# Work between two experts cut into single-engine steps, and the output accumulator begun by ScalarE and VectorE instead of GpSimd

## The chip, the core and the metric

The kernel runs on one core of a Trainium2 chip. Its engines work side by side, each through its own queue in order: TensorE (PE, matrix products; its weight loads are shown as PEld), VectorE (DVE), ScalarE (ACT), GpSimd (POOL) and SyncE (SP, which issues the transfers from HBM). PE writes its products to PSUM, from where ACT and DVE read them; everything else lies in SBUF. The metric is the device time of one execution in microseconds (us), taken as the median of several runs.

## What is computed

A two-layer block over 256 tokens of width 1024. Each layer is a convolution-and-retention mixer, a layer norm, a feed-forward part and a layer norm. The feed-forward part is dense in layer 0 and a mixture of 8 experts in layer 1, where each token goes to its best two experts. The change lies in the mixture alone:

```python
ALPHA = (2.0 * DEPTH) ** 0.25
D_MODEL, D_FF, N_EXPERTS, TOP_K = 1024, 3584, 8, 2

def moe_swiglu(h, router, w1, w3, w2):          # h: 256 x 1024
    logits = jnp.einsum('nd,de->ne', h, router)
    top_logit, top_e = lax.top_k(logits, TOP_K)
    gate = jax.nn.softmax(top_logit, axis=-1)
    ...                                         # tokens of each expert gathered into xe
    a = xe @ w1[e]
    c = xe @ w3[e]
    y = (jax.nn.silu(a) * c) @ w2[e]
    ...                                         # y times its gate, summed back to its token

x = layer_norm(ALPHA * x + moe_swiglu(x, ...), ln2_g, ln2_b)
```

## The kernel before

Everything is fp32. A product is made accurate by splitting each operand into a high part (an fp32r copy, `...h`) and a low part (the rest, `...l`) and adding three matmuls (`mm3`, L154 to L156: high by high, high by low, low by high). The function `parts` does the split: ACT copies the high part (L109), then DVE, or for a few weights POOL, subtracts it from the source (L110).

The mixture takes the time from about 477 us to 1471 us of the profiled execution. It has 8 experts of 7 blocks each; (e, b) is block b of expert e. A block handles 512 of the 3584 hidden columns and reads six weight tiles of 128x2048 from HBM (`raw`), each used as two splits (`wh`, `wl`, 128x1024): splits 0 to 3 are w1, 4 to 7 are w3, 8 to 11 are w2. A split feeds six matmuls of 512 columns. The third split of a block (split 2) has its low part made by POOL, all others by DVE. In program order a block is

- `a`: four calls of `up` over splits 0 to 3, among which the block before is finished: the activation `hh` after split 0 (`act`: silu on ACT, product on DVE), its transposes `ph` on PE after split 2 (`turn`), and its parts `hth`, `htl` after split 3 (`split_h`);
- `cc`: four calls of `up` over splits 4 to 7;
- `down_prev`: four calls of `down` over splits 8 to 11, for the block before, into the two PSUM tiles `y` of the expert (pool `py`, two buffers, so the next expert's `y` needs both to be read).

`W.take()` hands out a split and, with `LOOK = 2`, first writes the `parts` of the split two further on. So ACT and DVE are some splits ahead of PE in the program, and there are four buffers of splits (`SPL`): a split's high part can be written when PE is through with the split four before it.

No scheduler reorders anything (`manual_schedule`): each engine's queue is in the order in which the Python code emits its instructions. Work that belongs to no block is held in the list `side` as Python generators. `step()` runs the first of them up to its next `yield`. Before the change a block calls `step()` three times: after `a`, after the second split of `cc`, and after `cc`. The generators are

- `combine`, appended when an expert's last `down` is emitted, which is in block (e+1, 0): for each half h of `y` it takes the parts of `y` (`ysNh`, `ysNl`), multiplies with the selection matrix `PTx` on PE for both halves of the tokens (`put`, product `pc`, 2 matmuls each), and adds the gated product into `acc` on DVE (`add`, L772). It runs in blocks 1 and 2 of the next expert.
- `tokens_of(e+1)`, appended at block 2 of the odd experts 1, 3 and 5, for the next two experts: DVE builds the selection matrix `P` (4 instructions, L742), then four times PE gathers the tokens (`pg`, 8 matmuls of 256 columns, L751) and `parts` splits the product for the two experts (`gah`/`gal`, and `gbh`/`gbl` or `gch`/`gcl`), then PE transposes `P` (L760) and ACT copies it to `PTx`.

`pc`, `pg`, `pt` and `ph` share one PSUM pool of two buffers (`ptp`). At block (1, 0) the accumulator `acc` is begun: POOL adds the two parts of x (L873, two instructions of 128x1024) and ACT multiplies by ALPHA (L874).

## Time and profile before

| | |
|---|---|
| median of 3 runs | 1488.01 us (1486.11 to 1498.08) |
| the profiled execution | 1490.48 us |
| its span, first to last instruction | 1488.7 us |
| PE busy | 1438.5 us (97%) |
| PE weight loads busy | 1208.2 us (81%) |
| DVE busy | 1234.3 us (83%) |
| ACT busy | 973.8 us (65%) |
| POOL busy | 276.1 us (19%) |
| HBM read | 433.69 MB |

Times in the rows below are microseconds from the span's start. A matmul's duration overlaps the next one's, so PE's pace is read from one start to the next. "Idle before" is the time in which the engine had nothing to do ahead of an instruction, and the arrow names what ended it.

### The profile page before, as it was taken

To read this page: it belongs to the slowest core of one execution; us is meant where nothing else is said; L and a number is where in the kernel's file an instruction comes from. 1 tells how busy PE (TensorE), PEld (TensorE's weight loads), DVE (VectorE), ACT (ScalarE), POOL (GpSimd) and SP (SyncE) were. 2 spreads that over 40 slices of the span, in tenths; PEclk is the share of its full clock that TensorE was granted. 3 is DMA by queue.
4 is the path that set the end of the run, shared out by engine and by line. 5 is a ranking of instruction groups with operands and counts; after the bars stand their busy time and mean duration, and the time that the engine had idled before them with its cause. 6 is when DMAs were issued, how large, how long until landed. Compare 5 with 4: busy or idle time off the path is not lost. (4 is left out here: it accounts for less than half of the span.)

```text
span 1488.7 us, 19729 instructions
## 1 busy us (share of the span) xinstructions
PE 1438.5 (97%) x7385; PEld 1208.2 (81%) x7385; DVE 1234.3 (83%) x1401; ACT 973.8 (65%) x1153; POOL 276.1 (19%) x138
## 2 busy tenths in 40 slices
PE   9989999999987999999999999999999999999995
PEld 8859999998856887778878877888887888888884
DVE  7976455547987899889899998999899899999896
ACT  6334344434443877768877767777877777787773
POOL 5630000002844113111111111111111111111111
PEclk9999999999997999999999999999999999999998
DMA  9535544545547888979999997999998899999951
GB/s 368 208 113 227 194 175 183 211 161 182 183 164 310 311 312 336 343 300 356 382 342 378 367 356 302 368 371 352 378 376 304 342 376 354 363 373 370 353 216 59
DMA packets 62311, 436.10 MB, mean 293 GB/s; under 512 B 7040, under 2 KB 7424, under 8 KB 9856
## 3 DMA queue, kind: packets, MB, share of 16 engines
q1 hardware_dynamic: 61920, 434.24, 77.4%
q8 instruction: 60, 0.98, 0.3%
q10 hardware_dynamic: 288, 0.52, 0.1%
q14 instruction: 43, 0.35, 0.1%
HBM read 433.69 MB, written 1.05 MB: 292 GB/s over the span
## 5 line engine op out<-in xcount | busy, mean ns | idle before, releaser
L110 DVE TENSOR_TENSOR wl<-raw,wh 128x1024 fp32r<-128x1024 f32 (+1 forms) x704 | 880.5, 1289 | 61.2 <-ACT wh L109 35.8
L109 ACT CAST wh<-raw 128x1024 fp32r<-128x1024 f32 (+1 forms) x802 | 820.8, 1045 | 160.2 <-PE ac L156 94.7
L110 POOL TENSOR_TENSOR wl<-raw,wh 128x1024 fp32r<-128x1024 f32 x98 | 241.9, 2484 | 1107.3 <-ACT wh L109 1062.5
L155 PE MATMUL ac<-wl,gah 128*128 128x512 f32 x448 | 175.2, 391 | 2.8 <-DVE wl L110 2.3
L154 PE MATMUL ac<-wh,gah 128*128 128x512 f32 x448 | 177.4, 396 | 0.0
L154 PE MATMUL y<-wh,hth 128*128 128x512 f32 x440 | 172.8, 393 | 3.6 <-DVE ys1l L110 3.6
L155 PE MATMUL y<-wl,hth 128*128 128x512 f32 x440 | 172.0, 391 | 3.8 <-DVE wl L110 3.8
L156 PE MATMUL ac<-wh,gal 128*128 128x512 f32 x448 | 175.1, 391 | 0.0
L156 PE MATMUL y<-wh,htl 128*128 128x512 f32 x448 | 174.5, 390 | 0.0
L154 PE MATMUL wk<-xh,wh 128*128 128x256 f32 x512 | 145.4, 284 | 1.8 <-ACT wh L109 1.8
L156 PE MATMUL wk<-xh,wl 128*128 128x256 f32 x512 | 145.0, 283 | 0.2 <-DVE wl L110 0.2
L155 PE MATMUL wk<-xl,wh 128*128 128x256 f32 x512 | 144.7, 283 | 0.0
L391 DVE SCALAR_TENSOR_TENSOR wk<-u,colt,wk 128x256 f32<-128x256 f32 x209 | 99.8, 489 | 5.7
L154 PEld LDWEIGHTS y<-wh,hth 128*128 128x128 f32 x440 | 82.6, 188 | 24.3 <-DVE ys1l L110 6.6
L155 PEld LDWEIGHTS ac<-wl,gah 128*128 128x128 f32 x448 | 84.4, 188 | 21.4 <-DVE wl L110 3.6
L155 PEld LDWEIGHTS y<-wl,hth 128*128 128x128 f32 x440 | 82.6, 188 | 22.4 <-DVE wl L110 5.6
L154 PEld LDWEIGHTS wk<-xh,wh 128*128 128x128 f32 x512 | 97.4, 190 | 3.4 <-ACT wh L109 2.2
L156 PEld LDWEIGHTS wk<-xh,wl 128*128 128x128 f32 x512 | 99.1, 194 | 0.7 <-DVE wl L110 0.7
L156 PEld LDWEIGHTS ac<-wh,gal 128*128 128x128 f32 x448 | 84.3, 188 | 17.8
L156 PEld LDWEIGHTS y<-wh,htl 128*128 128x128 f32 x448 | 84.1, 188 | 17.4
L155 PEld LDWEIGHTS wk<-xl,wh 128*128 128x128 f32 x512 | 97.5, 190 | 0.9
L154 PEld LDWEIGHTS ac<-wh,gah 128*128 128x128 f32 x448 | 84.4, 188 | 16.6
(202 smaller groups left out, 2055.1 us busy)
## 6 DMA issues: line engine op xcount, KB each, us to landing
raw<-in_wm_dram SPq DMA_DIRECT2D x336, 1024.0 KB, 7.0
raw<-in_ws_dram SPq DMA_DIRECT2D x68, 1024.0 KB, 5.0
raw<-in_lnp_dram SPq DMA_DIRECT2D x4, 1024.0 KB, 5.0
raw<-in_ws_dram SPq DMA_DIRECT2D x8, 256.0 KB, 5.5
xf<-in_xT_dram SPq DMA_DIRECT2D x4, 256.0 KB, 4.7
x<-in_x_dram SPq DMA_DIRECT2D x1, 1024.0 KB, 7.5
mask<-in_mask_dram SPq DMA_DIRECT2D x1, 768.0 KB, 12.7
gn<-in_gnp_dram SPq DMA_DIRECT2D x2, 256.0 KB, 8.3
```

Source lines behind the costliest of these rows:

```text
L109: sc.copy(hi, src)
L110: (eng or v).tensor_tensor(lo, src, f32(hi), op=ALU.subtract)
L154: pe.matmul(o, a[0], b[0], start=first, stop=False, skip_group_check=True)
L155: pe.matmul(o, a[0], b[1], start=False, stop=False, skip_group_check=True)
L156: pe.matmul(o, a[1], b[0], start=False, stop=last, skip_group_check=True)
L391: v.scalar_tensor_tensor(d, u[:, cc, k:k + S], w[:, k:k + 1], o, op0=ALU.mult, op1=ALU.add)
```

## The change

The generators are cut at more places, so that a step emits work for PE alone, or for ACT and DVE alone. A block calls `step()` at six places: after `a`, after each of the first three splits of `cc`, after `cc`, and after the first split of `down_prev`. `combine` takes both halves of `y` apart in its first two steps and then alternates one `put` and one `add`. A gather step is cut between its matmuls and its `parts`. The accumulator is begun by a generator of its own, in four steps of 128x512 on ACT and DVE. `later_tokens` builds `P` in its first step and leaves the next one empty.

```diff
@@ gather
                                   skip_group_check=True)
+            yield
             for i in range(n):
                 parts(gs[i][0][:, k:k + 2, :], gs[i][1][:, k:k + 2, :], p[:, :, i, :])
             yield
...
                 pe.transpose(p[:, i, tok(t)], f32(P[:, t, 128 * i:128 * i + 128]), ident)
+        yield
         sc.copy(PT, p)
@@ combine
     def combine(y, PT, gate_of):
+
+        ys = []
         for h in range(2):
-            ys = split([128, 512], y[h], late[0], f"ys{h}")
+            ys.append(split([128, 512], y[h], late[0], f"ys{h}"))
             yield
-            ps = [put(ys, PT, t) for t in range(NT)]
+        for h in range(2):
             for t in range(NT):
-                add(ps[t], t, h, gate_of(t))
-            yield
+                p = put(ys[h], PT, t)
+                yield
+                add(p, t, h, gate_of(t))
+                yield
+
+    def start_acc():
+
+        for t in range(NT):
+            for h in range(2):
+                o = acc[:, t, half(h)]
+                sc.mul(o, f32(xn[0][:, t, half(h)]), ALPHA)
+                v.scalar_tensor_tensor(o, f32(xn[1][:, t, half(h)]), ALPHA, o, op0=ALU.mult, op1=ALU.add)
+                yield
...
+    def later_tokens(e0):
+        g = tokens_of(e0)
+        yield
+        yield
+        yield from g
@@ first gather, ahead of block (0, 0)
-    for _ in range(2):
+    for _ in range(4):
         next(g0)
@@ down_prev
             down(hp, q, W.take(), y, pb == 0, pb == NB - 1)
+            if q == 0:
+                step()
@@ block (1, 0)
-            for t in range(NT):
-                gp.tensor_tensor(acc[:, t, :], f32(xn[0][:, t, :]), f32(xn[1][:, t, :]), op=ALU.add)
-                sc.mul(acc[:, t, :], acc[:, t, :], ALPHA)
+            side.append(start_acc())
@@ blocks
-            side.append(tokens_of(e + 1))
+            side.append(later_tokens(e + 1))
...
             if not prev:
-                next(g0, 0)
+                next(g0, 0), next(g0, 0)
...
             up(cc, q, W.take(), got[e][0])
-            if q == 1:
+            if q < 3:
                 step()
         step()
```

What this does to the queues is shown at three places. The first is DVE in block (1, 1), from the parts `htl` of the block before to the activation `hh` of the next: `ys0l` and `ys1l` are the low parts of expert 0's result, `acc<-pc` the additions. Before:

```order
L110 TENSOR_TENSOR htl<-ph,hth 128x512
L110 TENSOR_TENSOR ys0l<-y,ys0h 128x512
L110 TENSOR_TENSOR wl<-raw,wh 128x1024 x2
L772 SCALAR_TENSOR_TENSOR acc<-pc,gate,acc 128x512 x2
L110 TENSOR_TENSOR wl<-raw,wh 128x1024 x2
L110 TENSOR_TENSOR ys1l<-y,ys1h 128x512
L110 TENSOR_TENSOR wl<-raw,wh 128x1024 x4
```

The same place of DVE after the change:

```order
L110 TENSOR_TENSOR htl<-ph,hth 128x512
L110 TENSOR_TENSOR ys0l<-y,ys0h 128x512
L110 TENSOR_TENSOR wl<-raw,wh 128x1024
L110 TENSOR_TENSOR ys1l<-y,ys1h 128x512
L110 TENSOR_TENSOR wl<-raw,wh 128x1024 x2
L774 SCALAR_TENSOR_TENSOR acc<-pc,gate,acc 128x512
L110 TENSOR_TENSOR wl<-raw,wh 128x1024 x2
L774 SCALAR_TENSOR_TENSOR acc<-pc,gate,acc 128x512
L110 TENSOR_TENSOR wl<-raw,wh 128x1024 x3
```

The low part `ys1l`, which frees the second `y` tile, moved up by three splits, and the two additions no longer stand together.

The second place is ACT in the gather of expert 1, blocks (1, 2) and (1, 3), from one `hth` on; `gah` and `gch` are the high parts of the gathered tokens. Before:

```order
L109 CAST hth<-ph 128x512
L109 CAST wh<-raw 128x1024 x2
L109 CAST gah<-pg 128x256
L109 CAST gch<-pg 128x256
L109 CAST wh<-raw 128x1024 x2
L109 CAST gah<-pg 128x256
L109 CAST gch<-pg 128x256
L109 CAST wh<-raw 128x1024 x5
L794 ACTIVATE hh<-ac 128x512
```

After the change, from the `hth` in block (1, 3):

```order
L109 CAST hth<-ph 128x512
L109 CAST wh<-raw 128x1024
L109 CAST gah<-pg 128x256
L109 CAST gch<-pg 128x256
L109 CAST wh<-raw 128x1024 x2
L109 CAST gah<-pg 128x256
L109 CAST gch<-pg 128x256
L109 CAST wh<-raw 128x1024 x2
L109 CAST gah<-pg 128x256
L109 CAST gch<-pg 128x256
L109 CAST wh<-raw 128x1024 x4
L809 ACTIVATE hh<-ac 128x512
```

The copies out of `pg` moved from blocks (1, 2) and (1, 3), two pairs each, to blocks (1, 3) and (1, 4), three pairs and one; on PE the eight matmuls of each pair now stand one turn (one split's six matmuls) ahead of where its copies are emitted.

The third place is the start of `acc`. On ACT before, around the boundary of blocks (0, 6) and (1, 0):

```order
L109 CAST wh<-raw 128x1024 x8
L874 ACTIVATE acc<-acc 128x1024 x2
L109 CAST wh<-raw 128x1024
L794 ACTIVATE hh<-ac 128x512
```

On DVE after the change, inside block (1, 0); ACT has a multiplication of 128x512 ahead of each, and POOL's two additions are gone from its queue:

```order
L110 TENSOR_TENSOR htl<-ph,hth 128x512
L795 SCALAR_TENSOR_TENSOR acc<-xl,acc 128x512
L110 TENSOR_TENSOR wl<-raw,wh 128x1024
L795 SCALAR_TENSOR_TENSOR acc<-xl,acc 128x512
L110 TENSOR_TENSOR wl<-raw,wh 128x1024
L795 SCALAR_TENSOR_TENSOR acc<-xl,acc 128x512
L110 TENSOR_TENSOR wl<-raw,wh 128x1024
L795 SCALAR_TENSOR_TENSOR acc<-xl,acc 128x512
L110 TENSOR_TENSOR wl<-raw,wh 128x1024 x5
```

The start moved from the block boundary, where POOL did it in two pieces, to four places between the splits 5 to 9 of block (1, 0), where DVE does it.

## Rows read from the trace of the kernel before

**Rows 1.** Windows of one block each: stretch, its us, busy PE, PEld, DVE, ACT, POOL; clock, DMA

```profile
1060.65:1077.47 16.82, 16.82 (x78) 13.91 (x77) 15.26 (x13) 13.43 (x15) 2.42 (x1) 1.00 0.94 375
575.91:595.99 20.08, 17.74 (x77) 13.67 (x76) 19.20 (x13) 13.69 (x15) 9.08 (x3) 1.00 0.83 311
595.99:613.91 17.92, 17.08 (x77) 13.83 (x76) 15.15 (x13) 14.67 (x17) 2.39 (x1) 1.00 0.95 356
1111.07:1129.59 18.52, 18.00 (x81) 14.58 (x80) 17.70 (x19) 14.24 (x17) 2.41 (x1) 1.00 0.93 343
1129.59:1151.69 22.10, 20.49 (x98) 16.39 (x97) 18.90 (x22) 14.20 (x19) 2.43 (x1) 1.00 0.78 288
1151.69:1171.97 20.28, 19.79 (x97) 16.11 (x96) 17.53 (x18) 14.74 (x20) 2.98 (x1) 1.00 0.81 312
1257.70:1275.61 17.91, 17.91 (x82) 14.58 (x81) 16.48 (x15) 13.40 (x15) 2.41 (x1) 1.00 0.92 334
```

**Rows 2.** Timeline of PE: start, us, line, operation; a gather's first matmul, the matmul behind it

```profile
643.19 0.28 PE L751 MATMUL pg<-P,xh 128*128 128x256 f32 x1
...
644.13 0.40 PE L154 MATMUL ac<-wh,gbh 128*128 128x512 f32 x1
```

**Rows 3.** Waits in the mixture: us in total, times, longest

```profile
PE y L155 <- DVE wl L110: 3.8, 6, 0.8
PE y L154 <- DVE ys1l L110: 3.6, 7, 0.5
```

**Rows 4.** Timeline of an undisturbed block: a low part on DVE, and PE's matmuls

```profile
1057.86 1.23 DVE L110 TENSOR_TENSOR wl<-raw,wh 128x1024 fp32r<-128x1024 f32 x1
1059.29 0.39 PE L154 MATMUL y<-wh,hth 128*128 128x512 f32 x1
1060.65 0.39 PE L154 MATMUL ac<-wh,gah 128*128 128x512 f32 x1
1060.88 0.39 PE L155 MATMUL ac<-wl,gah 128*128 128x512 f32 x1
1069.53 0.39 PE L155 MATMUL ac<-wl,gah 128*128 128x512 f32 x1
```

**Rows 5.** Timeline of DVE in that block

```profile
1062.01 4.43 DVE L110 TENSOR_TENSOR wl<-raw,wh 128x1024 fp32r<-128x1024 f32 x3 [0.26 <-ACT wh L109]
1066.37 0.68 DVE L110 TENSOR_TENSOR htl<-ph,hth 128x512 fp32r<-128x512 f32 x1
1066.97 3.49 DVE L110 TENSOR_TENSOR wl<-raw,wh 128x1024 fp32r<-128x1024 f32 x3
```

**Rows 6.** Timeline of ACT and DVE around a gather step in block (1, 2)

```profile
644.33 0.37 ACT L109 CAST gah<-pg 128x256 fp32r<-128x256 f32 x1 [4.65 <-PE pg L751]
644.74 0.42 DVE L110 TENSOR_TENSOR gal<-pg,gah 128x256 fp32r<-128x256 f32 x1 [1.09 <-ACT gah L109]
646.55 2.36 DVE L110 TENSOR_TENSOR wl<-raw,wh 128x1024 fp32r<-128x1024 f32 x2 [0.52 <-ACT wh L109]
```

**Rows 7.** Timeline of POOL, DVE and ACT around the start of `acc`

```profile
578.30 6.71 POOL L873 TENSOR_TENSOR acc<-xh,xl 128x1024 f32<-128x1024 f32 x2
577.27 8.82 DVE L110 TENSOR_TENSOR wl<-raw,wh 128x1024 fp32r<-128x1024 f32 x3 [0.25 <-ACT wh L109]
594.43 2.00 ACT L874 ACTIVATE acc<-acc 128x1024 f32<-128x1024 f32 x2
```

**Rows 8.** Timeline of DVE: an addition pair, two-input work in SBUF, a selection matrix

```profile
623.22 1.41 DVE L772 SCALAR_TENSOR_TENSOR acc<-pc,gate,acc 128x512 f32<-128x512 f32 x2
1483.27 2.06 DVE L1005 SCALAR_TENSOR_TENSOR acc<-acc,rsl,raw 128x512 f32<-128x512 f32 x3
472.99 0.88 DVE L742 TENSOR_SCALAR P<-iota,rk 128x128 fp32r<-128x128 f32 x4
```

**Rows 9.** Timeline of POOL: a split in an undisturbed block and in block (1, 3)

```profile
1060.68 2.42 POOL L110 TENSOR_TENSOR wl<-raw,wh 128x1024 fp32r<-128x1024 f32 x1 [14.09 <-ACT wh L109]
654.56 2.97 POOL L110 TENSOR_TENSOR wl<-raw,wh 128x1024 fp32r<-128x1024 f32 x1 [19.63 <-ACT wh L109]
```

## The prediction

> **What bounds the kernel now.** I read the windows of single blocks first [rows 1]. The undisturbed block, the first row, takes 16.82 us, all of it with PE at work and at clock 1.00, while DVE works 15.26 and ACT 13.43. So PE sets the pace, and a block that takes longer is longer by what PE was given to do in addition and by what it waited. The change adds and removes no matmul, so only waits can be won. I take the additional work out of the disturbed blocks at measured prices. A split is six matmuls and takes 1.36 (1059.29 to 1060.65) [rows 4], so one is 0.227; the four products `pc` of a block cost 0.91. A gather's eight matmuls cost 0.94 (643.19 to 644.13) [rows 2]. Four transposes cost 0.46, what 16.82 has left over 72 matmuls of 0.227. Then, by [rows 1]:
>
> - (5, 1): 18.52 - 16.82 - 0.91 = 0.79 waited
> - (5, 2), products and two gathers: 22.10 - 16.82 - 0.91 - 1.88 = 2.49
> - (5, 3), two gathers and `pt`: 20.28 - 16.82 - 1.88 - 0.46 = 1.12
> - (6, 2), products: 17.91 - 16.82 - 0.91 = 0.18; (6, 1) is like (5, 1), 0.79
> - (0, 6) 20.08 - 16.82 = 3.26 and (1, 0) 17.92 - 16.82 = 1.10, around the start of `acc`
>
> An odd and an even expert together wait 5.37. There are three such pairs (1 and 2, 3 and 4, 5 and 6), expert 7 has 0.97 without a gather, and `acc` has 4.36: 16.1 + 0.97 + 4.36 = 21.4 us in all. That is the most that the change can give, 1.4% of the time. The waits name the culprits: PE's `y` products wait for `ys1l`, once per expert, and for low parts `wl` [rows 3].
>
> **Why PE waits.** A low part is ready ahead of PE by a margin. In the undisturbed block DVE ends a `wl` at 1057.86 + 1.23 = 1059.09 and PE needs it at 1060.88: 1.79 [rows 4]. DVE makes one every 1.14 ((3.49 - 1.21) / 2) [rows 5] against PE's 1.36, so the margin regains 0.22 per split, up to 1.8. Each other DVE instruction takes its length off; each piece of extra PE work adds its own. After `htl` it is lowest: 1066.97 + 1.21 to 1069.53, 1.35 [rows 4, 5]. So a lump above 1.3 us on DVE stalls PE, and so does an engine that waits at its queue's head. The latter is the gather of before: ACT stood 4.65 before `gah`, since PE was some splits behind in the same program, and DVE 1.09 after it [rows 6].
>
> **The change, part by part.**
>
> *Combine.* The parts `ys0l` and `ys1l` now come in two turns before `down`, so the wait for `ys1l` goes. What they cost the margin: 1.35 after `htl`, less 0.60 for `ys0l` (the 0.60 that `htl` takes to the next start [rows 5]), plus 0.45 for the first product that PE does meanwhile, 1.20 for split 6; plus 0.22, less 0.60 for `ys1l`, 0.82 for split 7. An addition takes 0.66 (two end 1.41 after the first begins, the second running 0.75) [rows 8], and between two of them lie two splits (0.44) and a product (0.45), so the margin doesn't fall further. `P` takes 0.88 [rows 8] after split 9 of block 2, where it is back at 1.6. No wait is left: 0.
>
> Does an addition wait at the head of DVE's queue for its product? The product stands before split 6 on PE, the addition behind `wl` of split 8. DVE is there at the earliest 1.8 before PE needs split 8, 2.72 + 0.23 - 1.8 = 1.15 after PE is through with the product. No.
>
> *Gather.* With its matmuls a turn ahead, ACT still arrives first, but waits about 1 instead of 4.65. From PE's start on split 4, `gah` starts 0.20 later (644.13 to 644.33), `gal` 0.41 after that, the next `wl` 1.81 after that [rows 2, 6], and ends 1.21 on: 3.63. PE needs it (split 7) after three splits, one gather of 0.94 and 0.23, at 5.25: margin 1.62. Each further step stretches one interval of DVE from 1.14 to 1.14 + 1.81 = 2.95, against 1.36, and gains 0.94 on PE. Block 3 has three steps now: 1.62, 2.78 for split 8, 1.19 for split 9, 1.41, and 1.41 + 1.36 - 2.95 = -0.18 for split 11. A wait of 0.2, and I add 0.1 for the restart. What is late next is POOL's split of the next block. It has a margin of 0.5 (1060.68 + 2.42 to 1063.60, two splits behind 1060.88) [rows 4, 9], but with DVE's margin at about 0.6 there, DVE's `wl` runs 1.0 into its start, and POOL ends with it: in block (1, 3) POOL took 2.97 instead of 2.42 in that way [rows 9]. That makes 0.35 and 0.1 of restart. Together 0.8 per odd expert, 2.3 in all. Bounds: 0, if the steps overlap better than I chain them, and 13.7, if all twelve steps wait as the longest did before, 0.8 idle [rows 3] and 0.34 of restart and lost overlap. I take 2.3, nearest to rows 6, which have the same chain.
>
> *Accumulator.* POOL's two additions take 6.71, and the three `wl` of DVE beside them 8.82, 2.94 each instead of 1.14 [rows 7]; ACT's two multiplications, 2.00, hold up the cast for POOL's next split. Both go, 4.36 with them. New are four DVE instructions of two SBUF operands, 0.66 each by ((2.06 - 0.74) / 2) [rows 8], and up to 2.9 for one that meets a POOL instruction, as the `wl` in [rows 7]; POOL has one split per block, early, so they lie clear. Four turns in a row cost 0.66 - 0.22 = 0.44 of margin each: 1.35 - 0.66 = 0.69 for split 6, then 0.25, -0.19, and again below zero: two waits of 0.2 to 0.3 and two restarts of 0.1, 0.8 in all. ACT's four multiplications, half as long as those of [rows 7], 0.5 each, fit its idle time.
>
> Here the Trainium skill speaks against the change. "Perfetto Trace Analysis", section Optimizing Scalar/DVE Operations, says that where DVE is saturated, work should move off it, to Scalar or even GPSIMD; this moves the other way. The trace bears it out in part: DVE's idle time in a block is 16.82 - 15.26 = 1.56 [rows 1], less than the 2.64 that it is given. What that would make of the time is the third rival.
>
> *The rest.* The first gather's order on each engine is unchanged; the fallback for crowded experts has no row in the trace. The weights' transfers keep their order; they are hidden, no wait of PE names one.
>
> *Sum.* 21.4 - 2.3 - 0.8 = 18.3 off. The profiled execution, 1490.5 with a span of 1488.7, becomes 1472.2; the median stands 2.5 below it, 1488.0 - 18.3 = 1469.7.
>
> **The rivals.**
>
> *The gather still stalls.* For it: rows 6 show how one step blocks three queues in turn, and three steps now fall in one block instead of two. Against: the longest part of that wait, 4.65, was the distance in the program. If the twelve steps cost between what they cost now (about 2.7 per odd expert, 8.1) and 13.7 instead of 2.3, the time is 1475.5 to 1481; I set 1477.
>
> *No new waits at all.* If steps overlap, all 21.4 are won: 1466.6. Against: the chain of [rows 6] is three engines long.
>
> *The accumulator overloads DVE.* If POOL's additions were not what held DVE's `wl`, the 4.36 would stay and DVE's 2.64 come on top: 1488.0 - (21.4 - 4.36) + 2.3 + 2.6 = 1475.9. Against: the three `wl` are slow exactly while POOL adds [rows 7].
>
> *The pace of the transfers takes over.* Undisturbed blocks already move 375 GB/s at a share of 0.94 [rows 1]. If 375 were the ceiling over the whole mixture, gains would be lost in the stretches that need more; but a pair with its combines and gathers now needs 14 blocks' weights in 14 x 16.82 + 7.9, 3% below 375. A quarter of the gain lost would give 1474.
>
> *DVE waits for PE (the slower side).* Place: the 28 additions and 12 gather steps, each now behind PE work that is emitted one turn ahead. If the products come later than DVE, each wait is up to one turn, 1.36, 54 in all, of which DVE's idle time (1.56 a block [rows 1], some 20 blocks) hides 31: 1470 + 23 = 1493. It decides from 0.46 uncovered per step on (18.3 / 40). Against: 1.15 us of lead worked out above.
>
> That the change does not do what it says is excluded by the queues' order.
>
> **How the numbers follow.** Forecast (1467.5 to 1473): 0.58. Gather still stalls (up to 1481): 0.19. No new waits: 0.10. Accumulator: 0.04. Transfers: 0.04. Slower side: 0.05. A measurement tells about 1% (14.9 us, 1473.1) from no change. Forecast and no new waits lie beyond that but for a small tail: faster 0.66. Within 1%: the gather's case, accumulator, transfers, part of the last and the tail, 0.30. Slower by over 1% needs 33 us over the forecast, 0.8 per step uncovered: 0.04. The range reaches from 1466, all waits gone, to 1479, most of the gather's case; about 0.15 lies outside.
>
> **What would show it.** Right: PE's wait for `ys1l` is gone; blocks 1 and 2 of an expert take 17.7 (16.82 + 0.91), block 3 of an odd one 19.7 to 20.0 (three gathers, one wait), (0, 6) 16.8; ACT's idle time ahead of `gah` is near 1; a wait of 0.2 to 0.5 is left in blocks 3 and 4 of the odd experts and in (1, 0). Wrong: waits of about 1 in (5, 3), or DVE waiting for `pc`. The prediction falls if blocks without side work are no longer 16.8.

## The result, and the profile after

The changed kernel takes 1471.11 us in the median of 4 runs (1469.57 to 1474.45), the kernel before 1487.53 in runs beside it. The ratio is 0.9884 with a 95% interval of 0.9858 to 0.9909: 1.2% faster, as forecast (1469.7, range 1466 to 1479).

The profiled execution took 1474.45 us, its span is 1472.6, 16.1 shorter than before's. Not all of the difference between two spans belongs to the change, so I compare one stretch in both: from PE's start on block (0, 1) to its start on block (7, 6), which holds all that the change touches but the steps of the first gather. Windows of this stretch, with the columns of [rows 1], before:

```profile
491.07:1446.56 955.49, 941.87 (x4270) 772.03 (x4268) 868.89 (x788) 740.15 (x803) 139.53 (x56) 1.00 0.92 349
```

and after:

```profile
493.64:1430.52 936.88, 935.82 (x4269) 773.16 (x4268) 860.89 (x792) 740.01 (x805) 133.23 (x54) 1.00 0.93 356
```

The stretch is 18.61 us shorter, with TensorE's granted clock at 1.00 in both. The sum of the prediction was 18.3. PE's busy time is now within 1.1 us of the stretch, and DVE has less busy time than before although it was given the accumulator: its low parts no longer stand beside POOL's additions, and the three later matrices `P` take 0.86 us each, where they took 3.03 beside POOL's split. The same views of single blocks as in [rows 1], after: the undisturbed (5, 5), then (0, 6), (1, 0), (5, 1) to (5, 4), (6, 2):

```profile
1174.84:1191.65 16.81, 16.81 (x77) 13.90 (x76) 15.27 (x13) 13.39 (x15) 2.42 (x1) 1.00 0.99 381
578.46:595.25 16.79, 16.79 (x77) 13.91 (x76) 15.25 (x13) 13.40 (x15) 2.42 (x1) 1.00 0.95 353
595.25:612.63 17.38, 17.32 (x77) 13.75 (x76) 16.71 (x17) 15.05 (x19) 2.41 (x1) 1.00 0.96 362
1100.71:1118.43 17.72, 17.72 (x81) 14.66 (x80) 17.05 (x17) 14.15 (x17) 2.41 (x1) 1.00 0.92 331
1118.43:1136.13 17.70, 17.70 (x81) 14.66 (x80) 17.28 (x20) 13.42 (x15) 2.51 (x1) 1.00 0.97 364
1136.13:1156.12 19.99, 19.99 (x102) 16.67 (x101) 16.44 (x19) 14.52 (x20) 2.42 (x1) 1.00 0.89 320
1156.12:1174.84 18.72, 18.56 (x90) 15.17 (x88) 17.19 (x16) 14.58 (x19) 2.82 (x1) 1.00 0.89 351
1242.96:1260.68 17.72, 17.72 (x82) 14.65 (x80) 16.79 (x16) 13.40 (x15) 2.53 (x1) 1.00 0.95 352
```

The reader takes out the extra PE work as the prediction did. Blocks 1 and 2 of an expert are 16.81 + 0.91: no wait. (5, 3) has three gathers, 16.81 + 2.82 = 19.63, so 0.36 was waited; (5, 4) has one and the transposes, 16.81 + 0.94 + 0.46 = 18.21, so 0.51. (1, 0) waits 0.57. Two of the waits of the mixture (us in total, times, longest) that are left:

```profile
PEld y L155 <- DVE wl L110: 2.2, 6, 0.5
...
PE ac L155 <- POOL wl L110: 1.0, 4, 0.5
```

The wait for `ys1l` [rows 3] is gone. Where the 0.36 and the 0.51 lie is seen in the timeline of block (5, 3) and its end. ACT's casts of the three gather steps (in brackets the idle time before them):

```profile
1143.19 0.37 ACT L109 CAST gah<-pg 128x256 fp32r<-128x256 f32 x1 [0.81 <-PE pg L751]
1144.06 0.37 ACT L109 CAST gch<-pg 128x256 fp32r<-128x256 f32 x1 [0.49 <-DVE gal L110]
...
1146.89 0.37 ACT L109 CAST gah<-pg 128x256 fp32r<-128x256 f32 x1 [0.56 <-PE pg L751]
1148.13 0.37 ACT L109 CAST gch<-pg 128x256 fp32r<-128x256 f32 x1 [0.88 <-DVE gal L110]
...
1150.59 0.38 ACT L109 CAST gah<-pg 128x256 fp32r<-128x256 f32 x1 [0.18 <-PE pg L751]
1152.22 0.37 ACT L109 CAST gch<-pg 128x256 fp32r<-128x256 f32 x1 [1.26 <-DVE gal L110]
```

ACT waits 0.8 and less for PE, where [rows 6] had 4.65. Its second cast, `gch`, waits for DVE's `gal`, and longer from step to step, so that a step costs ACT 1.30, 1.44 and 1.44 of idle time in all. DVE's low parts behind the last of them, POOL's split, and PE's matmuls on these parts:

```profile
1153.57 3.50 DVE L110 TENSOR_TENSOR wl<-raw,wh 128x1024 fp32r<-128x1024 f32 x3 [0.52 <-ACT wh L109]
...
1156.52 2.82 POOL L110 TENSOR_TENSOR wl<-raw,wh 128x1024 fp32r<-128x1024 f32 x1 [17.95 <-ACT wh L109]
...
1154.51 0.39 PE L154 MATMUL y<-wh,hth 128*128 128x512 f32 x1
1154.85 0.50 PE L155 MATMUL y<-wl,hth 128*128 128x512 f32 x1
...
1158.85 0.39 PE L154 MATMUL ac<-wh,gbh 128*128 128x512 f32 x1
1159.39 0.50 PE L155 MATMUL ac<-wl,gbh 128*128 128x512 f32 x1 [0.16 <-POOL wl L110]
```

From L154 to L155 PE takes 0.23 when it does not wait; here it takes 0.34 at split 11 and 0.54 at POOL's split. POOL runs from 1156.52 to 1159.34, 2.82 instead of 2.42, since DVE's third `wl` lies beside its start. The matmul behind each of the two waits also starts 0.1 late (1155.19 and 1159.72, 0.34 and 0.33 behind the one that waited, instead of 0.23).

### The profile page after: what moved, and what is told of

The parts are those of the page before. It is cut to its first block, busy times and chain, and to the rows that moved or that the text cites. A ratio compares the mean times of both kernels' runs of the same rounds, so it can differ in the third digit from the quotient of the medians.

```text
span 1472.6 us, 19730 instructions
## 1 busy us (share of the span) xinstructions
PE 1436.3 (98%) x7385; PEld 1211.4 (82%) x7385; DVE 1226.3 (83%) x1405; ACT 973.6 (66%) x1155; POOL 269.6 (18%) x136
## 3 DMA queue, kind: packets, MB, share of 16 engines
HBM read 433.69 MB, written 1.05 MB: 295 GB/s over the span
## 5 line engine op out<-in xcount | busy, mean ns | idle before, releaser
L154 PE MATMUL ac<-wh,gah 128*128 128x512 f32 x448 | 177.4, 396 | 0.0
L155 PE MATMUL ac<-wl,gah 128*128 128x512 f32 x448 | 174.9, 390 | 0.5 <-POOL wl L110 0.5
L155 PE MATMUL y<-wl,hth 128*128 128x512 f32 x440 | 171.7, 390 | 0.1
L154 PE MATMUL y<-wh,hth 128*128 128x512 f32 x440 | 171.4, 389 | 0.0
L154 PE MATMUL wk<-xh,wh 128*128 128x256 f32 x512 | 145.6, 284 | 0.7 <-ACT wh L109 0.7
L155 PE MATMUL wk<-xl,wh 128*128 128x256 f32 x512 | 144.9, 283 | 0.0
L154 PEld LDWEIGHTS wk<-xh,wh 128*128 128x128 f32 x512 | 97.5, 190 | 2.4 <-ACT wh L109 1.3
L155 PEld LDWEIGHTS ac<-wl,gah 128*128 128x128 f32 x448 | 84.4, 188 | 17.7 <-POOL wl L110 0.9
L156 PEld LDWEIGHTS ac<-wh,gal 128*128 128x128 f32 x448 | 84.2, 188 | 17.9
L155 PEld LDWEIGHTS wk<-xl,wh 128*128 128x128 f32 x512 | 97.6, 191 | 0.9
L156 PEld LDWEIGHTS y<-wh,htl 128*128 128x128 f32 x448 | 84.1, 188 | 17.4
L154 PEld LDWEIGHTS ac<-wh,gah 128*128 128x128 f32 x448 | 84.5, 189 | 16.6
L155 PEld LDWEIGHTS y<-wl,hth 128*128 128x128 f32 x440 | 82.6, 188 | 18.8 <-DVE wl L110 1.9
L154 PEld LDWEIGHTS y<-wh,hth 128*128 128x128 f32 x440 | 82.6, 188 | 17.1
```

The lines of the kernel that those rows point to most:

```text
L154: pe.matmul(o, a[0], b[0], start=first, stop=False, skip_group_check=True)
L155: pe.matmul(o, a[0], b[1], start=False, stop=False, skip_group_check=True)
L156: pe.matmul(o, a[1], b[0], start=False, stop=last, skip_group_check=True)
```

## The experiments

A table first. "Stretch" is PE's time from block (0, 1) to (7, 6) as above; it leaves out what varies ahead of the mixture, so it tells apart what the medians can't.

| kernel | stretch | against the changed kernel | median, us | ratio to before |
|---|---|---|---|---|
| before | 955.49 | +18.61 | 1487.5 to 1488.6 | 1 |
| changed | 936.88 | 0 | 1471.11 | 0.9884 (0.9858 to 0.9909) |
| changed, again | 936.84 | 0.0 | 1468.44 | 0.9867 (0.9845 to 0.9890) |
| accumulator as before | 940.56 | +3.7 | 1473.74 | 0.9889 (0.9853 to 0.9926) |
| gather joined | 941.34 | +4.5 | 1474.09 | 0.9899 (0.9860 to 0.9938) |
| combine as before | 944.27 | +7.4 | 1477.40 | 0.9913 (0.9883 to 0.9943) |
| spread, one place late | 935.84 | -1.0 | 1468.34 | 0.9852 (0.9824 to 0.9880) |
| lumps added | 940.55 | +3.7 | 1471.56, one run | |
| combine joined | 937.41 | +0.5 | 1473.13, one run | |
| accumulator on POOL, cut | 938.66 | +1.8 | 1470.35, one run | |
| gather spread | 934.74 | -2.1 | 1467.07 | 0.9855 (0.9832 to 0.9877) |
| POOL forms added | 937.91 | +1.0 | 1471.67, one run | |
| places alone | 949.29 | +12.4 | 1481.80, one run | |

**The accumulator as before.** This takes back one part:

```diff
-            side.append(start_acc())
+            for t in range(NT):
+                gp.tensor_tensor(acc[:, t, :], f32(xn[0][:, t, :]), f32(xn[1][:, t, :]), op=ALU.add)
+                sc.mul(acc[:, t, :], acc[:, t, :], ALPHA)
```

> The changed kernel, but the accumulator is begun as before: two GpSimd additions and two ScalarE multiplications in one piece ahead of block (1, 0). Theory (GpSimd's additions hold up VectorE's low parts while they run, and ScalarE's multiplications hold up a cast): block (0, 6) goes back from 16.79 to 20.1 us and (1, 0) from 17.38 to 17.9, all others stay; the three low parts beside the additions take 2.9 each again; the time is 1471.1 + 3.8 = 1474.9. Rival (the accumulator's work on VectorE is what costs in the changed kernel, since VectorE is nearly full): (1, 0) falls to 16.8, (0, 6) rises by less than 0.6, the time is 1471 or less.

Windows of (0, 6) and (1, 0):

```profile
574.28:594.31 20.03, 17.68 (x77) 13.68 (x76) 19.20 (x13) 13.67 (x15) 9.08 (x3) 1.00 0.78 297
594.31:612.25 17.94, 17.09 (x77) 13.83 (x76) 15.15 (x13) 14.68 (x17) 2.39 (x1) 1.00 0.93 355
```

The timeline of DVE, its low parts beside POOL's additions:

```profile
575.64 8.83 DVE L110 TENSOR_TENSOR wl<-raw,wh 128x1024 fp32r<-128x1024 f32 x3 [0.25 <-ACT wh L109]
```

Both blocks are as in [rows 1], the three low parts take 8.83 as in [rows 7], and all else stays but (1, 2), which takes 17.70 instead of 17.83: this part of the change is worth 3.24 + 0.56 = 3.8 by the two blocks, 3.7 by the stretch, of 4.36 that the prediction gave to it before its own 0.8. The rival is out: DVE, with a busy time of 16.71 in (1, 0) of the changed kernel, carries the work at 0.57 of waiting.

**The gather joined.** The casts and subtractions go back to the step of their matmuls; an empty step keeps the matmuls where they were:

```diff
                                   skip_group_check=True)
-            yield
             for i in range(n):
                 parts(gs[i][0][:, k:k + 2, :], gs[i][1][:, k:k + 2, :], p[:, :, i, :])
             yield
+            yield
@@
-        yield
         sc.copy(PT, p)
+        yield
```

> The changed kernel, but the gather's casts and subtractions are issued in the same step as their matmuls; the matmuls stay at the same places of the block, and the copy of PT comes with its transposes. It isolates 'one engine's turn at a time' from 'more places, further apart'. Theory (ScalarE and VectorE wait at the head of their queues for the matmuls, since they are ahead of TensorE): ScalarE's idle time before a gah grows from about 1 to over 2 us, the low part behind a step comes one split earlier in need, its margin falls from 1.6 to about 0.3 at the first step and below zero at the following ones; blocks 3 and 4 of an odd expert, 38.7 together, become 40 to 42.5, and the time 1475 to 1482. Rival (only the spacing over six places matters): blocks 3 and 4 stay within 0.3 of 19.98 and 18.70, and the time within 1470 to 1472.

Windows of (5, 3) and (5, 4):

```profile
1133.94:1155.28 21.34, 20.55 (x102) 16.65 (x100) 16.71 (x19) 14.91 (x21) 2.41 (x1) 1.00 0.86 303
1155.28:1174.14 18.86, 18.76 (x90) 15.17 (x88) 16.96 (x16) 14.31 (x18) 2.98 (x1) 1.00 0.85 338
```

The timeline of ACT, the casts in (5, 3):

```profile
1141.00 0.37 ACT L109 CAST gah<-pg 128x256 fp32r<-128x256 f32 x1 [1.75 <-PE pg L751]
...
1144.70 0.37 ACT L109 CAST gah<-pg 128x256 fp32r<-128x256 f32 x1 [0.57 <-PE pg L751]
...
1148.40 0.37 ACT L109 CAST gah<-pg 128x256 fp32r<-128x256 f32 x1 [0.18 <-PE pg L751]
```

The two blocks take 40.2, the low end of the theory's 40 to 42.5 (the median of 1474.09 is just under its 1475); the rival's 38.7 is out. The theory was right on the first step (ACT idles 1.75 instead of 0.81) and wrong on the next ones, where ACT waits 0.57 and 0.18 ahead of `gah`, and 0.88 and 1.26 ahead of `gch`, as in the changed kernel. So the turn between matmuls and parts is worth 1.5 per odd expert, lost at the first step of a block, and not a wait more per step.

**The combine as before.** The order within `combine` and its places are those of before, the rest as changed:

```diff
-        ys = []
         for h in range(2):
-            ys.append(split([128, 512], y[h], late[0], f"ys{h}"))
+            ys = split([128, 512], y[h], late[0], f"ys{h}")
             yield
-        for h in range(2):
-            for t in range(NT):
-                p = put(ys[h], PT, t)
-                yield
-                add(p, t, h, gate_of(t))
-                yield
+            yield
+            ps = [put(ys, PT, t) for t in range(NT)]
+            for t in range(NT):
+                add(ps[t], t, h, gate_of(t))
+            yield
+            yield
+        yield
+        yield
```

> The changed kernel, but the combine runs as before at the places of before: ys0, then its two products with their additions two places on, ys1 two places on, its two products with their additions in the next block; the gather's steps and the accumulator stay as changed. Theory (TensorE waits for ys1l because that part is made only right before the down products need its buffer): the wait for ys1l is back, 0.8 per expert; block 1 of each expert is 18.5 instead of 17.7, block 2 within 0.2 of 17.7; seven experts give +5.5 to +7, the time is 1477 to 1478. Rival (the four additions lump by lump on VectorE were the cost, whatever the place of ys1): block 2 is longer by as much as block 1, 0.4 to 0.8 each.

Windows of (5, 1) and (5, 2):

```profile
1113.31:1131.86 18.55, 18.03 (x81) 14.58 (x80) 17.50 (x17) 14.24 (x17) 2.42 (x1) 1.00 0.96 349
1131.86:1149.78 17.92, 17.92 (x82) 14.58 (x80) 17.00 (x19) 13.44 (x15) 2.41 (x1) 1.00 0.97 358
```

PE's wait in the whole mixture (us in total, times, longest):

```profile
PE y L154 <- DVE ys1l L110: 3.8, 7, 0.7
```

The wait for `ys1l` is back in all seven experts. Block 1 is longer by 0.83, block 2 by 0.22, together 1.05 and 7.4 in all: the late `ys1l` makes four fifths of it. Most of the rest is in block 2, at the second of two products in a row, whose weight load waits 0.3 for `htl`: as the code has it, that part has to be made before the PSUM buffer of `ph` is free for the product. So the combine is 7.4 of the 18.6; the accumulator is 3.7, and the 7.5 that are left are the gather's and, as is shown further down, those of the place where `P` is built.

**The combine joined.** Only the turn between a product and its addition is taken away:

```diff
                 p = put(ys[h], PT, t)
-                yield
                 add(p, t, h, gate_of(t))
                 yield
+                yield
```

> The changed kernel, but each addition of the combine is issued in the same step as its product, with an empty step behind; the products, the splits, the gather and the accumulator stay at their places. Theory (VectorE is 1.1 us behind a product with the turn between, which is about the 1.14 us of the low part that no longer lies between): VectorE reaches the addition just as the product ends, it waits 0 to 0.3, and blocks 1 and 2 of an expert stay within 0.3 of 17.7; the time is 1471 to 1473. Rival (the turn is what the combine gains by): VectorE waits 0.5 to 1 per addition, blocks 1 and 2 become 18.2 or more, seven experts give +7, 1478.

Blocks 1 and 2 stay at 17.7 in all seven experts, and DVE waits for a product 1.0 us in 6 waits, 0.2 at the longest. Only block 3 of an odd expert is longer, 20.17 instead of 19.98, 0.5 in all. So in the combine it is the place of `ys1` that counts, not the turn between product and addition, and the slower rival (DVE at the head of its queue, waiting for PE) does not bite even without that turn.

**The places alone.** The kernel before, with the three more places for a step and nothing else:

```diff
         for q in range(4):
             down(hp, q, W.take(), y, pb == 0, pb == NB - 1)
+            if q == 0:
+                step()
@@
-            if q == 1:
+            if q < 3:
                 step()
```

> The kernel before with one part of the change alone: side work gets a turn at six places of a block instead of three; the pieces themselves are not cut, and the accumulator is as before. Theory (the places bring ys1l earlier, but put uncut pieces closer together): the wait for ys1l is gone; block 1 of an expert holds the whole combine, 16.82 + 1.81 + 0.3 to 0.6 = 19.1, block 2 of an even one is 16.8, together 35.9 against 36.5; in block 2 of an odd one all four gathers lie a split apart, 16.82 + 3.76 + 0.46 + 2 to 4 us of waits = 23 to 25, block 3 is 16.8, so an odd expert's three blocks take 59 to 61 against 60.9; in all 3 to 6 us below the kernel before, 1482 to 1485. Rival (the places are what the change gains by, the cutting is not needed): the three blocks of an odd expert take 57 or less, and the time is 1476 or less.

Windows of (5, 1) to (5, 3) and (6, 2):

```profile
1104.98:1123.83 18.85, 18.85 (x85) 15.34 (x84) 18.18 (x19) 14.26 (x17) 2.42 (x1) 1.00 0.90 339
1123.83:1147.84 24.01, 22.43 (x113) 17.86 (x112) 19.95 (x26) 15.97 (x24) 2.70 (x1) 1.00 0.69 261
1147.84:1164.84 17.00, 17.00 (x77) 13.84 (x76) 16.35 (x14) 13.35 (x15) 2.97 (x1) 1.00 0.97 386
...
1250.93:1267.76 16.83, 16.83 (x78) 13.91 (x76) 15.86 (x14) 13.41 (x15) 2.69 (x1) 1.00 0.98 383
```

The odd expert's three blocks take 59.86, the even one's two 18.85 + 16.83 = 35.7, at the short end of the theory's range; the stretch is 6.2 shorter than before's, a third of the gain. Block 1 holds the whole combine and waits 0.2 (18.85 - 16.81 - 1.82), so the `ys1l` wait is cured by the place alone. Block (5, 2) holds all four gathers and waits 24.01 - 16.81 - 3.76 - 0.46 = 2.98: uncut pieces a split apart, and some 0.6 of it at POOL's split, which lies beside the building of `P` and takes 2.70. Cutting and distance together take that away; the joined gather tells what the cutting alone is worth, 1.5.

**The margin.** VectorE work that changes nothing, in undisturbed blocks:

```diff
+    LUMPS = {(2, 4): 1, (2, 6): 2, (4, 4): 3, (4, 6): 4, (6, 4): 1}
+    def lump(n):
+        for _ in range(n):
+            o = acc[:, 0, half(0)]
+            v.scalar_tensor_tensor(o, o, 1.0, o, op0=ALU.mult, op1=ALU.max)
...
         step()
+        lump(LUMPS.get((e, b), 0))
         cc = new_ac()
```

and in (6, 4) three more single ones, behind the second and fourth split of `cc` and the second of `down`.

> The changed kernel with VectorE instructions added that leave the accumulator as it is (a maximum of a 128x512 half of acc with itself, some 0.66 us each), in blocks that were undisturbed (16.8 us): one in block (2, 4), two in (2, 6), three in (4, 4), four in (4, 6), each lump at one place, right behind htl's turn; and in (6, 4) four single ones, two splits apart. Theory (the margin of 1.35 us that low parts have there, regained by 0.22 per split): (2, 4) and (2, 6) stay at 16.8, (4, 4) waits 1.98 - 1.35 + 0.1, so 17.5, (4, 6) waits 2.64 - 1.35 + 0.1, so 18.2; (6, 4) with the same 2.64 us as (4, 6) stays at 16.8 to 16.9. Rival (what counts is VectorE's idle time in a block, 1.56 us): 16.8, 16.8, 17.2 and 17.9, and (6, 4) takes 17.9 like (4, 6).

Windows of (2, 4), (2, 6), (4, 4), (4, 6), (6, 4), and of (6, 5), which has no added work:

```profile
783.16:799.97 16.81, 16.81 (x77) 13.90 (x76) 15.66 (x14) 13.40 (x15) 2.42 (x1) 1.00 0.94 361
816.76:833.73 16.97, 16.97 (x77) 13.82 (x76) 16.09 (x15) 13.41 (x15) 2.41 (x1) 1.00 0.97 358
1027.26:1045.30 18.04, 17.12 (x77) 13.79 (x76) 17.11 (x16) 13.39 (x15) 2.42 (x1) 1.00 0.85 331
1062.12:1080.58 18.46, 17.12 (x77) 13.83 (x76) 17.49 (x17) 13.39 (x15) 2.42 (x1) 1.00 0.93 341
1274.15:1290.96 16.81, 16.81 (x77) 13.90 (x76) 16.14 (x17) 13.40 (x15) 2.41 (x1) 1.00 0.94 356
1290.96:1308.35 17.39, 17.11 (x77) 13.83 (x76) 16.73 (x14) 13.39 (x15) 3.31 (x1) 1.00 0.93 358
```

One, two, three and four at once cost 0, 0.16, 1.23 and 1.65. The same four set apart cost nothing in their block. That is the margin and not the block's idle time: by that rival (4, 6) and (6, 4) would be alike, 17.9. Two sizes were off. (4, 4) and (4, 6) wait 0.5 and 0.3 more than I expected: DVE lost 2.77 for four (they start at 1068.43, the `wl` behind them at 1071.20), which is 1.4 over the margin of 1.35, and the restart took 0.2 and not 0.1; the block (4, 4) begins with 0.3 less margin (its first `wl` takes 2.47, that of (4, 6) 2.16). And the four single ones are not free: DVE comes into (6, 5) late, lies beside POOL's split, which takes 3.31 instead of 2.42, and PE waits 0.58 for it. It is the wait that (5, 4) of the changed kernel shows.

**More distance.** First both generators were spread:

```diff
-        yield from g
+        for i, _ in enumerate(g):
+            yield
+            if i in (2, 4, 6):
+                yield
@@ start_acc
                 yield
+                if (t, h) in ((0, 0), (0, 1)):
+                    yield
```

> The changed kernel with more distance: an empty step behind each of the gather's first three pairs of matmuls and parts (so blocks 3 and 4 of an odd expert get two gathers each, instead of three and one), and an empty step behind the first two of the four pieces that begin the accumulator. Theory (the margin regains 0.22 us per split, so work three splits apart costs 0.22 less per step and never uses the margin up): block 3 becomes 16.82 + 1.88 = 18.7, block 4 16.82 + 1.88 + 0.46 = 19.2, together 37.9 against 38.7, three times; block (1, 0) 17.1 instead of 17.38; the time is 1471.1 - 2.4 - 0.3 = 1468.4. Rival (the waits left are no matter of margin but of each step's own chain): nothing changes within 0.5, 1471; or the transposes in the same block as two gathers make a new wait, 1471 to 1473.

The empty steps of the gather stand one place later than this text says, behind the second to the fourth piece, since `later_tokens` has the first piece's matmuls in the first round of the loop. So block 3 kept three gathers: 19.73, block 4 18.37, block 5 17.07, together 0.36 less per odd expert. The accumulator gained nothing: (1, 0) took 16.93 instead of 17.38, but (1, 1) 18.16 instead of 17.73. The margin that it used came due a block later, where the combine needs it; that is our reading of the two blocks, no run shows it apart. The next run has the gather's empty steps where they were meant to be, and the accumulator as changed:

```diff
-        yield from g
+        for i, _ in enumerate(g):
+            yield
+            if i in (1, 3, 5):
+                yield
```

> The changed kernel with one change: an empty step behind the parts of each of the gather's first three pieces, so that block 3 of an odd expert gets two gathers, block 4 two gathers and the transposes. In the run e4_spread the empty steps stood one place later, behind the second to the fourth piece, and block 3 kept three gathers. Theory (margin): block 3 takes 16.82 + 1.88 = 18.7, block 4 19.2, together 37.9 against 38.7, block 5 16.8; three odd experts give -2.5; the time is 1468.6, 0.9983 of the changed kernel's. Rival (a wait of some 0.3 behind the transposes, as block 5 had in e4_spread, comes with every order): -0.3 to -1.2 in all, 1470 to 1471.

Windows of (5, 3) to (5, 5):

```profile
1131.02:1149.77 18.75, 18.75 (x94) 15.80 (x92) 16.17 (x17) 14.28 (x19) 2.41 (x1) 1.00 0.87 331
1149.77:1168.99 19.22, 19.22 (x98) 16.19 (x96) 17.01 (x18) 14.37 (x19) 2.61 (x1) 1.00 0.87 335
1168.99:1185.78 16.79, 16.79 (x77) 13.91 (x76) 15.24 (x14) 13.77 (x16) 2.42 (x1) 1.00 0.97 383
```

Less 16.81, the gathers and the transposes, 0.06 and 0.07 are left in the two blocks. The stretch is 2.1 shorter than the changed kernel's. The medians, 1467.07 against 1468.44 beside it, agree in sign, but their ratios to before overlap; the blocks are what shows it. This version beats both kernels.

**The changed kernel again** stood beside it, for the comparison:

> The changed kernel itself, beside e8_gather_spread on the same chip, so that the two can be compared: 1471.1, blocks (e, 3) and (e, 4) of odd experts 19.98 and 18.7, (1, 0) 17.4. If its time before the first expert's block varies by some us, as it did between the two profiled executions (2.5 us), that part is not the change's.

Its stretch is the changed kernel's within 0.04, its time 2.7 less. In the window of the first 200 us of the changed kernel the granted clock is 0.98:

```profile
0.00:200.00 200.00, 193.63 (x1206) 168.38 (x1207) 138.82 (x246) 90.38 (x139) 57.48 (x39) 0.98 0.58 218
```

The same window of the same kernel in this run, at clock 1.00:

```profile
0.00:200.00 200.00, 193.86 (x1240) 169.81 (x1241) 139.23 (x248) 90.75 (x140) 57.47 (x39) 1.00 0.59 223
```

PE's first matmul of the mixture starts at 479.69 in the one and at 474.14 in the other: one program reached the mixture 5.6 us apart. Over all profiled executions that start lies between 473.9 and 488.0; the latest is that of the combine as before, with 0.96 in the same window.

**Who holds VectorE.** The accumulator in the four steps of the change, but on POOL:

```diff
+        o = None
         for t in range(NT):
             for h in range(2):
+                if o is not None:
+                    sc.mul(o, o, ALPHA)
                 o = acc[:, t, half(h)]
-                sc.mul(o, f32(xn[0][:, t, half(h)]), ALPHA)
-                v.scalar_tensor_tensor(o, f32(xn[1][:, t, half(h)]), ALPHA, o, op0=ALU.mult, op1=ALU.add)
+                gp.tensor_tensor(o, f32(xn[0][:, t, half(h)]), f32(xn[1][:, t, half(h)]), op=ALU.add)
                 yield
+        sc.mul(o, o, ALPHA)
+        yield
```

> The changed kernel, but the four pieces that begin the accumulator, one per step in block (1, 0), are GpSimd additions of 128x512 each, ScalarE's multiplication of a piece one step behind it. It keeps the change's cutting and places, and takes back only the engine. Theory (VectorE's low parts stand while GpSimd reads its two operands, whatever the size of a piece): 5.4 us of delay, the three low parts of 8.8 us against 3.4, are now spread over four steps, 1.35 each against 0.22 that the margin regains; 4 x 1.13 - 1.35 = 3.2 of waits, (1, 0) takes 20.0 instead of 17.38, (0, 6) stays at 16.8; the time is 2.6 above the changed kernel's. Rival (the additions cost because they came in one lump, or because ScalarE waited for them): (1, 0) takes 17.4 or less.

The window of block (1, 0):

```profile
589.44:608.70 19.26, 17.78 (x78) 13.67 (x76) 18.59 (x13) 15.34 (x19) 11.34 (x5) 1.00 0.80 300
```

The timeline of POOL's additions in it, and of DVE's low parts beside them:

```profile
591.84 8.97 POOL L797 TENSOR_TENSOR acc<-xh,xl 128x512 f32<-128x512 f32 x4
...
590.80 6.63 DVE L110 TENSOR_TENSOR wl<-raw,wh 128x1024 fp32r<-128x1024 f32 x3 [0.25 <-ACT wh L109]
...
597.95 10.76 DVE L110 TENSOR_TENSOR wl<-raw,wh 128x1024 fp32r<-128x1024 f32 x8
```

The block waits 2.4, against 0.57 with the work on ACT and DVE, and the rival (17.4 or less) is out: the engine matters. My 20.0 was too long, for two reasons that the rows show. The cutting had no effect on POOL, whose queue holds nothing between the pieces, so the four ran in one go; and they held DVE up by 3.8 (6.63 for three and 10.76 for eight, against 4.43 [rows 5] and 9.17, which eight took in block (4, 6) of the lumps), not 5.4. The 5.4 was itself too much: at that place of a block three low parts take 4.43 without any addition, since the first of them lies beside POOL's own split and takes 2.16, so the two additions of the kernel before held DVE up by 8.82 - 4.43 = 4.4 [rows 5, 7]. ScalarE waits for POOL here too, 0.7 once, but DVE is nowhere idle from its first low part to the end of the block; the next run takes ScalarE out of it. The last experiment puts two instructions of three kinds behind `htl` in undisturbed blocks:

```diff
+    def extra(eb):
+        for h in range(2):
+            if eb == (2, 5):
+                o = acc[:, 0, half(0)]
+                gp.tensor_tensor(o, o, acc[:, 0, half(1)], op=(ALU.add, ALU.subtract)[h])
+            if eb == (4, 5):
+                o = acc[:, 0, half(h)]
+                gp.tensor_scalar(o, o, 1.0, None, op0=ALU.mult)
+            if eb == (6, 5):
+                o = acc[:, 0, half(h)]
+                sc.mul(o, o, 1.0)
```

> The changed kernel with two instructions of 128x512 added at the place behind htl in three undisturbed blocks (16.8 us); they leave the accumulator as it is, but for rounding: in (2, 5) GpSimd adds a half of acc to the other and takes it off again (two operands), in (4, 5) GpSimd multiplies by 1.0 (one operand), in (6, 5) ScalarE multiplies by 1.0. Theory (two engines that read two operands each hold one another up): in (2, 5) the low parts beside GpSimd take 2 to 3 us each instead of 1.2, VectorE is delayed by 1.9 to 2.7, as by the four additions of e7_acc_pool_cut (3.8) or the two of the kernel before (5.4), and the block takes 17.4 to 18.2; with one operand GpSimd holds nothing, (4, 5) stays at 16.8; ScalarE's work is inside its idle time, (6, 5) 16.8 to 16.9. Rival (any work of GpSimd in SBUF holds VectorE): (4, 5) is as long as (2, 5), and its low parts are as slow.

DVE's three low parts beside the two instructions, in (2, 5), (4, 5) and (6, 5):

```profile
804.05 6.64 DVE L110 TENSOR_TENSOR wl<-raw,wh 128x1024 fp32r<-128x1024 f32 x3 [0.24 <-ACT wh L109]
...
1049.03 5.26 DVE L110 TENSOR_TENSOR wl<-raw,wh 128x1024 fp32r<-128x1024 f32 x3 [0.25 <-ACT wh L109]
...
1293.03 4.43 DVE L110 TENSOR_TENSOR wl<-raw,wh 128x1024 fp32r<-128x1024 f32 x3 [0.24 <-ACT wh L109]
```

With two operands on POOL DVE loses 2.21 and the block takes 17.84; with one it loses 0.83, which the margin covers (16.81); beside ACT's the three lose nothing; behind `htl` DVE waits 0.93 for a cast, which the margin covers (16.79). So the theory held on the blocks, but "one operand holds nothing" was wrong.

## Why the prediction was right, point by point

| the prediction's step | predicted | measured |
|---|---|---|
| undisturbed block stays | 16.8 | 16.81 |
| combine: blocks 1 and 2 | 17.7, no wait | 17.72 and 17.70 |
| gather: block 3 of an odd expert | 19.7 to 20.0 | 19.99 |
| ACT's idle time before `gah` | near 1 | 0.81, 0.56, 0.18; with `gch` 1.30, 1.44, 1.44 |
| gather's waits left, per odd expert | 0.8 | 0.36 + 0.51 = 0.87 |
| (0, 6) | 16.8 | 16.79 |
| waits left at the accumulator | 0.8 | 0.57 in (1, 0), 0.1 in (1, 2) |
| waits of the kernel before, in all | 21.4 | 21.9 (18.6 won, 3.3 left) |
| gain in the mixture | 18.3 | 18.61 |

**The margin** was the step on which the rest stood, and it held split by split, not only in the sum. For splits 7 to 10 of block 3 its chain gave 1.62, 2.78, 1.19 and 1.41; in (5, 3) the low parts are ready 1.68, 2.85, 1.29 and 1.52 before PE begins on them. For split 11 it gave -0.18; the trace has PE waiting 0.11 there, and then POOL's split late by 0.31, where 0.35 was forecast. The lumps show the margin by itself. One detail was off: in an undisturbed block it is not lowest after `htl` (1.35) but a little lower at split 3 (1.23), the first low part behind POOL's split.

**The combine** was right for the reason given. What the text could not separate the runs did: the place of `ys1` carries it (the places alone take 0.75 of an even expert's 0.97), the turn between product and addition is worth 0.5 us in the whole kernel.

**The gather** was right in its sum. That ACT would wait "near 1" at each step holds for its two casts together (1.30, 1.44, 1.44); ahead of `gah` alone the wait shrinks, since DVE falls behind and `gch` then waits for `gal` instead.

Of the kernel before, one wait was put in the wrong place. The prediction gives (5, 2) 2.49 us for products and two gathers, and names only `ys1l` and `wl` [rows 3]. But PE also waited for `htl`, 2.6 us in the whole mixture, once in block 2 of each of the experts 1, 3 and 5. The timelines of DVE and PE before, in (1, 2):

```profile
632.18 3.03 DVE L742 TENSOR_SCALAR P<-iota,rk 128x128 fp32r<-128x128 f32 x4
...
639.86 0.50 PE L767 MATMUL pc<-ys1h,PTx 128*128 128x512 f32 x1 [0.85 <-DVE htl L110]
```

`P` was built at the start of block 2, beside POOL's split (632.51 to 634.93), and took 3.03 instead of the 0.88 of [rows 8]. That made `htl` late, and with it the PSUM buffer for the second `pc` (`ptp` has two buffers, and `ph` holds one until `htl` is made). With the matmul behind it this cost 1.1 per odd expert, against 0.2 in an even one, which builds no `P`: some 2.8 in all. The change builds `P` behind split 9, where it takes 0.86 (in (5, 2)), and the run with the combine as before shows that this is what cures it: there (5, 2) takes 17.92, like block 2 of an even expert before. So the parts are 7.4 for the combine, 3.7 for the accumulator, 4.5 for the gather's turn and some 2.8 for the place of `P`, 18.4 of 18.6. The forecast was not hurt by the wrong place, because it took the waits of before from whole blocks and let all of them go.

**The accumulator** was right in sign and close in size, 3.8 net against 4.36 - 0.8 = 3.6. Its premise, that POOL's additions hold DVE's low parts, was an inference from one place of the trace; now three more places show it. "2.94 each instead of 1.14" was misread: the first of the three takes 2.16 without any addition, and only the other two were held. With the delay of 4.4 that is left the margin gives the wait as well: less 1.35, and with 0.2 of restart, it makes 3.2, and (0, 6) waited 3.26; the 2.21 of the last experiment make 1.06, and (2, 5) waited 1.03.

The Trainium skill ("Perfetto Trace Analysis", section Optimizing Scalar/DVE Operations) says that with a saturated DVE, moving some work to Scalar or even GPSIMD "may make sense", and right behind it, which the prediction left out, that GPSIMD and DVE share an SBUF read port, so that moving it between those two "might not help". The runs fit the second statement, not the first: DVE's busy time in (1, 0) went up from 15.15 [rows 1] to 16.71, and the block got shorter.

**The rivals.** The gather's stall and the overloaded DVE would have shown as waits of 1 and more in (5, 3) and (1, 0); there are none. The pace of the transfers does not bind: undisturbed blocks move 381 GB/s now at an unchanged 16.81. DVE waiting for PE would show as idle time before `acc<-pc`: joined to its product, the addition waited 0.2 at most. "No new waits at all" was wrong in the kernel tested, but the spread version comes within 0.4 us of it in the gather's blocks: with 0.13 per odd expert left, what stood in the way was distance, not the length of the chain.

**What was not in the sum.** The time before the mixture. The two profiled executions reached it 2.5 us apart with the same work ahead of it, so the spans differ by 16.1 and not by 18.6, and the medians of the changed kernel in two sets of runs are 1471.1 and 1468.4, 16.4 and 19.7 below before's. That the first set came within 1.4 of 1469.7 is in part luck; the stretch is what the forecast is to be held against. A range for a median of this kernel needs some 3 us for that alone.

## What to carry to other kernels

Where an engine runs ahead of the bound engine by a margin, cost an inserted instruction against that margin at its place, not against the engine's idle time: 2.7 us at once cost 1.65, and in four pieces two splits apart nothing in their block and 0.58 in the next. Emit first what frees a buffer that the bound engine needs soon (here `ys1`, 0.8 us per expert). Give work that passes through three engines a turn for each where they would wait in a row (1.5 per odd expert in the gather); where they would not, as between product and addition of the combine, it is worth little. Keep a short instruction away from the place where another engine's longer one would hold it (`P`, 0.88 or 3.03). Compare one marked stretch of two traces rather than two spans, when the clock ahead of it varies.

## What the runs showed of the hardware

GpSimd work that reads SBUF delays VectorE instructions with two SBUF operands: two additions of 128x512 cost three low parts 2.21 us, four cost 3.8, and two of 128x1024 4.4 (8.82 against 4.43 [rows 5, 7]). GpSimd is delayed in turn: an addition of 128x512 took 2.2 to 2.3 beside VectorE's low parts, and 1.27 at the end of the kernel. The Trainium skill ("SBUF — State Buffer", section Who interferes with whom) says that a VectorE instruction with two SBUF inputs contends with a GpSimd instruction that reads SBUF; the runs agree. What I had not expected is that the one-operand multiplication on GpSimd, which ran 4.0 us for two, cost only 0.83: less than half of what the additions (4.5 us for two) cost. Why is open. Nor is it work with two tiles alone that is held: one of the four instructions that build `P`, which reads one tile and a column, took 2.44 beside POOL's split in the kernel before, the other three 0.28 each.

A TensorE that waits loses a little more than the wait: the matmul that had waited took 0.50 instead of 0.39, and the next one started 0.34 behind it instead of 0.23. Of the 1.65 that the four lumps cost, 0.2 is not explained by the late low part; this is half of it.
